# Two-layer diffusion backbone with PEER experts: decoding by 16-bit folds, gate one-hots by four-token comparisons

## Chip, cores and metric

The kernel runs on one core of a Trainium2 chip. The metric is device time in microseconds (us) of one execution; the time before is the median of three runs. The five engines of the core are called PE (matrix products, with PEld for its weight loads), DVE (vector), ACT (scalar and activation), POOL (general purpose) and SP (issues most DMAs).

## What is computed

Two layers over 512 latent and 256 context tokens of width 1024. Each layer has an attention and recurrent mixer, which the change leaves alone, and then a feed-forward part in which each token picks, for each of 8 heads, 16 of 16,384 experts:

```python
def peer_ffn(h, w_query, subkeys1, subkeys2, expert_u, expert_v):
    q = (h @ w_query).reshape(B, L, PEER_HEADS, 2, PEER_HALF)
    s1 = jnp.einsum('blhd,kd->blhk', q[..., 0, :], subkeys1)
    s2 = jnp.einsum('blhd,kd->blhk', q[..., 1, :], subkeys2)
    v1, i1 = lax.top_k(s1, PEER_TOPK)        # 16 of 128 rows
    v2, i2 = lax.top_k(s2, PEER_TOPK)        # 16 of 128 columns
    cand_score = v1[..., :, None] + v2[..., None, :]
    cand_index = i1[..., :, None] * N_KEYS + i2[..., None, :]
    top_score, top_pos = lax.top_k(cand_score, PEER_TOPK)
    expert_idx = jnp.take_along_axis(cand_index, top_pos, axis=-1)
    gates = jax.nn.softmax(top_score, axis=-1)
    ...
    act = gelu(einsum('td,ted->te', h_blk, expert_u[i_blk]))
    out = einsum('te,ted->td', g_blk * act, expert_v[i_blk])
```

Layer 0 does this for 4 blocks of 128 latent tokens and 2 of context tokens, layer 1 for the 4 latent blocks alone.

## The kernel before

**Two ways to the experts.** Some token blocks are *dense*: all 16,384 experts are computed for them with matrix products, and a gate matrix that is zero nearly everywhere picks what counts (the 4 latent blocks in layer 0, 3 of them in layer 1). The other blocks are *gathered*: POOL fetches one row of the expert table per token and step (L1285), and DVE multiplies it (L1297, and L1310 for the second table). Gather steps are strewn among all the rest.

**Choosing and decoding (`topk2`).** For each block, DVE finds the best 16 of 54 candidate pairs for each head and has their positions (`txf`). `decode` turns positions into expert numbers, two heads a call, four calls a block, 40 calls in the program: ACT spreads the positions (`tte`, L1220), DVE compares them with 0 to 53 (`toe`, L1225), multiplies by the candidates' numbers, which gives one nonzero in each row of 54 (`toh`, 16-bit integers, L1226), and sums each of the 32 rows (`tef`, L1227).

**The gate stage.** For a dense block, `gprep` transposes the expert numbers, split into row and column, and the gates into `gT` (rows 0, 1 and 2 of `T3`). `gstep` then takes four tokens at a time: a one-hot `o1` of the row number, a one-hot `o2` of the column number times the gate, and a product `o2` by `o1` for each token on PE (`g_ps`, L1558), which ACT copies out (`Gs`, L1560) and SP writes to memory. `o1` is made by DVE in one comparison over four tokens on odd steps (L1547), and on even steps by ACT (four times Abs into `ohd`, L1552, and one Relu, L1553). `o2` is made by DVE, one instruction per token with comparison and multiplication in one (L1555). The trace calls both tiles `oh`. There are 128 steps in layer 0 and 96 in layer 1, with three buffers of each one-hot and two of `g_ps`.

**What runs beside it.** In the same stage PE computes the first table's product for the dense blocks (`u_ps`, L158): per step `ustep`, SP loads `raw`, ACT rounds it to `uhi` (L1470), DVE subtracts to get `ulo` (L1471), PE does 24 matrix products, ACT applies Gelu (`ga`, L1476). A function `merge` spreads these steps, the gate steps, the decoding of the next block and gather steps evenly, and a scheduler then orders each engine's instructions before the program runs. Each engine works through its list in that fixed order. Behind the gate stage comes the second table's product (`pa` and `po`, L158).

Of the kernel before, what the change touches and what calls it, by code (L numbers as in the profile page):

```python
# [10 lines left out]
F32 = mybir.dt.float32  # L11
# [5 lines left out]
AF = mybir.ActivationFunctionType  # L17
ALU = mybir.AluOpType
# [83 lines left out]
def body(ctx: ExitStack, tc: tile.TileContext, I: dict, out: bass.AP):  # L102
    nc = tc.nc
    V, A, G, PE, SP = nc.vector, nc.scalar, nc.gpsimd, nc.tensor, nc.sync
    mul, add, sub = ALU.mult, ALU.add, ALU.subtract
# [7 lines left out]
    def K(name):  # L113
        o, n = COFF[name]
        return cst[:, o:o + n]
# [1051 lines left out]
    def topk2(pool, rp, tvx, res):  # L1167
        v, ix = tvx
        vv = v.rearrange("p (h f) k -> p h f k", f=2)
        w = {}  # L1170

        def prep():
            ixf = pool.tile([128, 16, 16], F32, name="tixf")
            V.tensor_copy(ixf, ix)
            iv = ixf.rearrange("p (h f) k -> p h f k", f=2)
            i1s = pool.tile([128, 8, 16], F32, name="ti1")
            V.tensor_scalar(i1s, iv[:, :, 0, :], 128.0, None, op0=mul)
            cd = w["cd"] = pool.tile([128, 8, NCAND], F32, name="tcd")
            ci = pool.tile([128, 8, NCAND], F32, name="tci")
            at = 0  # L1180
            for a0, a1, n in SEGS:
                na = a1 - a0
                for dst, x1, x2 in ((cd, vv[:, :, 0], vv[:, :, 1]), (ci, i1s, iv[:, :, 1])):
                    G.tensor_tensor(dst[:, :, at:at + na * n].rearrange("p h (a b) -> p h a b", b=n),
                                    x1[:, :, a0:a1, None].to_broadcast([128, 8, na, n]),
                                    x2[:, :, None, 0:n].to_broadcast([128, 8, na, n]), op=add)
                at += na * n
            w["ci"] = pool.tile([128, 8, NCAND], I16, name="tcj")
            A.copy(w["ci"], ci)

        def top():
            w["tv"] = pool.tile([128, 8, 16], F32, name="ttv")
            w["tx"] = pool.tile([128, 8, 16], U32, name="ttx")
            w["c2"] = pool.tile([128, 8, NCAND], F32, name="tc2")
            for h in range(8):
                V.max(out=w["tv"][:, h, 0:8], in_=w["cd"][:, h, :])

        def top2():
            for h in range(8):
                V.max_index(out=w["tx"][:, h, 0:8], in_max=w["tv"][:, h, 0:8], in_values=w["cd"][:, h, :])  # L1200

        def top3():
            for h in range(8):
                V.match_replace(out=w["c2"][:, h, :], in_to_replace=w["tv"][:, h, 0:8], in_values=w["cd"][:, h, :],  # L1204
                                imm_value=NEG)

        def top4():
            for h in range(8):
                V.max(out=w["tv"][:, h, 8:16], in_=w["c2"][:, h, :])

        def top5():
            for h in range(8):
                V.max_index(out=w["tx"][:, h, 8:16], in_max=w["tv"][:, h, 8:16], in_values=w["c2"][:, h, :])  # L1213
            w["txf"] = pool.tile([128, 8, 16], F32, name="ttxf")
            V.tensor_copy(w["txf"], w["tx"])
            w["ef"] = pool.tile([128, 128], F32, name="tef")

        def spread(h):
            te = w["te", h] = pool.tile([128, 2, 16, NCAND], BF, name="tte", bufs=2)
            A.copy(te, w["txf"][:, h:h + 2, :, None].to_broadcast([128, 2, 16, NCAND]))  # L1220

        def decode(h):
            oe = pool.tile([128, 2, 16, NCAND], BF, name="toe", bufs=1)
            oh = pool.tile([128, 2, 16, NCAND], I16, name="toh", bufs=1)
            V.tensor_tensor(oe, io16[:, None, None, :].to_broadcast([128, 2, 16, NCAND]), w["te", h], op=ALU.is_equal)  # L1225
            V.tensor_tensor(oh, oe, w["ci"][:, h:h + 2, None, :].to_broadcast([128, 2, 16, NCAND]), op=mul)  # L1226
            V.tensor_reduce(w["ef"][:, 16 * h:16 * h + 32].rearrange("p (h j) -> p h j", j=16), oh,  # L1227
                            axis=AX.X, op=add)

        def gates():  # L1230
            g = rp.tile([128, 8, 16], F32, name="gate")
            tv = w["tv"]
            V.tensor_tensor(g, tv, tv[:, :, 0:1].to_broadcast([128, 8, 16]), op=sub)
            A.activation(g, g, AF.Exp)
            sm = pool.tile([128, 8], F32, name="tsm")
            V.tensor_reduce(sm, g, axis=AX.X, op=add)
            V.reciprocal(sm, sm)
            V.tensor_tensor(g, g, sm[:, :, None].to_broadcast([128, 8, 16]), op=mul)
            res["g"] = g.rearrange("p h k -> p (h k)")

        def index():
            eidx = res["e"] = rp.tile([128, 128], I32, name="eidx")
            V.tensor_copy(eidx, w["ef"])

        return [prep, top, top2, top3, top4, top5, lambda: spread(0), gates, lambda: (spread(2), decode(0)), lambda: (spread(4), decode(2)),
                lambda: (spread(6), decode(4)), lambda: decode(6), index]

    def ffn_rows(L, r, mk):
# [80 lines left out]
    def tail(L, cat, last, ro, need_ctx):  # L1329
# [61 lines left out]
        op = eo.enter_context(tc.tile_pool(name=f"op{l}", bufs=1, side="right"))  # L1391
# [109 lines left out]
        wp = e1.enter_context(tc.tile_pool(name=f"pt{l}", bufs=1, side="right"))  # L1501
# [35 lines left out]
        def gstep(q, b, t0):  # L1537
            T3 = R[b]["T3"]
            if t0 % GTC == 0:
                R["Gs"] = gsp.tile([128, 128, GTC], F32, name="Gs")  # L1540
            Gs = R["Gs"]
            gp = pp.tile([128, 4, 128], F32, name="g_ps", tag="q_ps", bufs=2)
            o1 = wp.tile([128, 4, 128], F32, name="oh1", bufs=3)
            o2 = wp.tile([128, 4, 128], F32, name="oh2", bufs=3)
            io = K("iota")
            if (t0 // 4) % 2:
                V.tensor_tensor(o1, io[:, None, :].to_broadcast([128, 4, 128]),  # L1547
                                T3[:, 0, t0:t0 + 4, None].to_broadcast([128, 4, 128]), op=ALU.is_equal)
            else:
                od = wp.tile([128, 4, 128], F32, name="ohd", bufs=2)  # L1550
                for t in range(4):
                    A.activation(od[:, t, :], io, AF.Abs, scale=-1.0, bias=T3[:, 0, t0 + t:t0 + t + 1])  # L1552
                A.activation(o1, od, AF.Relu, scale=-1.0, bias=1.0)  # L1553
            for t in range(4):
                V.tensor_scalar(o2[:, t, :], io, T3[:, 1, t0 + t:t0 + t + 1], T3[:, 2, t0 + t:t0 + t + 1],  # L1555
                                op0=ALU.is_equal, op1=mul)
            for t in range(4):
                PE.matmul(gp[:, t, :], o2[:, t, :], o1[:, t, :], start=True, stop=True)  # L1558
            tl = t0 % GTC
            A.copy(Gs[:, :, tl:tl + 4], gp.rearrange("p t i -> p i t"))  # L1560
            if tl + 4 == GTC:
                SP.dma_start(gscr[(128 * q + t0) // GTC], Gs)

        seq = []
        for q, b in enumerate(dn):
            if q == 0:
                seq += topk2(wp, wp, tk[b], R[b])
            if q == 0 and gl:
                for c in gl:
                    seq += topk2(wp, gr, tk[c], R[c]) + [lambda c=c: gather(c)]  # L1570
            nxt = topk2(wp, wp, tk[dn[q + 1]], R[dn[q + 1]]) if q + 1 < nd else []
            gs = [lambda b=b: gprep(b)] + [lambda q=q, b=b, t=t: gstep(q, b, t) for t in range(0, 128, 4)]
            k = len(gs) // (len(nxt) + 1)
            for i, f in enumerate(gs):
                seq.append(f)
                if nxt and i % k == k - 1:
                    seq.append(nxt.pop(0))
            seq += nxt
# [202 lines left out]
```

## Time and profile before

| what | value |
|---|---|
| three runs | 4742.24, 4747.82 (median), 4757.47 us |
| the profiled execution | 4753.17 us, of which 4751.4 us span |
| busy share of the span | PE 90%, DVE 76%, ACT 41%, POOL 29% |
| gate stage of layer 0, first to last `g_ps` | 1121.1 to 1471.0 us |
| gate stage of layer 1 | 3616.0 to 3905.2 us |

The shares are means over stages with different limits, so the view to read is busy time by stretch: an engine that is busy through a whole stretch holds the others up there, and one that has gaps can take more work at no cost. Instructions overlap by some hundredths of a us on DVE and ACT, so the cost of one is read best from the distance between two starts in the timeline. The clock granted to PE is given as a share of 2.4 GHz.

### The profile page before, as it was taken

To read this page: it belongs to the slowest core of one execution; us is meant where nothing else is said; L and a number is where in the kernel's file an instruction comes from. 1 tells how busy PE (TensorE), PEld (TensorE's weight loads), DVE (VectorE), ACT (ScalarE), POOL (GpSimd) and SP (SyncE) were. 2 spreads that over 40 slices of the span, in tenths; PEclk is the share of its full clock that TensorE was granted. 3 is DMA by queue.
4 is the path that set the end of the run, shared out by engine and by line. 5 is a ranking of instruction groups with operands and counts; after the bars stand their busy time and mean duration, and the time that the engine had idled before them with its cause. 6 is when DMAs were issued, how large, how long until landed. Compare 5 with 4: busy or idle time off the path is not lost. (4 is left out here: it accounts for less than half of the span.)

```text
span 4751.4 us, 85354 instructions
## 1 busy us (share of the span) xinstructions
PE 4288.6 (90%) x32715; PEld 3568.5 (75%) x32715; DVE 3619.3 (76%) x7842; ACT 1952.0 (41%) x3407; POOL 1366.7 (29%) x1256
## 2 busy tenths in 40 slices
PE   6998688877999999988899989868898999999999
PEld 4664576766787887767687778457678997899998
DVE  3457675899997888877788746766589967888885
ACT  3355343436674232222222234644336763333332
POOL 0201002442222345555455221200222102244441
PEclk8999898998999999999999999989899999999999
DMA  6656415435779999988898632651525769999995
GB/s 242 236 178 196 103 39 192 160 124 186 253 264 330 333 321 330 316 302 295 288 330 317 236 123 85 203 132 30 175 90 192 255 249 332 345 330 336 333 326 209
DMA packets 576904, 1106.71 MB, mean 233 GB/s; under 512 B 145328, under 2 KB 358000, under 8 KB 566768
## 3 DMA queue, kind: packets, MB, share of 16 engines
q1 hardware_dynamic: 465904, 698.56, 43.0%
q0 software_dynamic: 110592, 402.70, 23.6%
q8 instruction: 257, 4.21, 0.4%
q14 instruction: 151, 1.24, 0.1%
HBM read 960.37 MB, written 140.74 MB: 232 GB/s over the span
## 5 line engine op out<-in xcount | busy, mean ns | idle before, releaser
L158 PE MATMUL u_ps<-phi,uhi 128*128 128x512 f32 (+1 forms) x2048 | 765.1, 374 | 65.2 <-ACT ga L1476 48.4
L1285 POOL DMA_INDIRECT u<-in_u,eidx x384 | 485.7, 1265 | 1173.1 <-DVE u L1297 836.0
L158 PE MATMUL u_ps<-phi,ulo 128*128 128x512 f32 (+1 forms) x2048 | 757.3, 370 | 34.1 <-DVE ulo L1471 34.1
L158 PE MATMUL u_ps<-plo,uhi 128*128 128x512 f32 (+1 forms) x2048 | 753.3, 368 | 0.0
L1285 POOL DMA_INDIRECT u<-in_v,eidx x384 | 517.7, 1348 | 518.1 <-DVE gacc L1310 434.5
L1470 ACT CAST uhi<-raw 128x1024 fp32r<-128x1024 f32 x256 | 269.0, 1051 | 933.9 <-PE u_ps L158 546.6
L158 PE MATMUL pa<-vhi,whi 128*128 128x512 f32 x1536 | 601.5, 392 | 10.5 <-ACT whi L149 10.5
L158 PE MATMUL pa<-vlo,whi 128*128 128x512 f32 x1536 | 601.2, 391 | 0.0
L158 PE MATMUL pa<-vhi,wlo 128*128 128x512 f32 x1536 | 600.9, 391 | 0.0
L1297 DVE SCALAR_TENSOR_TENSOR u<-u,gh 128x1024 f32<-128x1024 f32 x384 | 468.3, 1230 | 120.2 <-DMA u<-in_u,eidx 112.4
L1310 DVE SCALAR_TENSOR_TENSOR gacc<-u,gw,gacc 128x1024 f32<-128x1024 f32 x381 | 488.4, 1282 | 93.3 <-DMA u<-in_v,eidx 89.8
L158 PEld LDWEIGHTS u_ps<-phi,uhi 128*128 128x128 f32 x2048 | 392.6, 192 | 120.2 <-ACT ga L1476 58.6
L158 PEld LDWEIGHTS u_ps<-phi,ulo 128*128 128x128 f32 x2048 | 391.3, 191 | 81.0 <-DVE ulo L1471 38.9
L158 PEld LDWEIGHTS u_ps<-plo,uhi 128*128 128x128 f32 x2048 | 392.2, 192 | 44.2
L1471 DVE TENSOR_TENSOR ulo<-raw,uhi 128x1024 fp32r<-128x1024 f32 x256 | 313.8, 1226 | 143.4 <-ACT uhi L1470 139.6
L149 ACT CAST whi<-w 128x512 fp32r<-128x512 f32 (+1 forms) x256 | 145.5, 568 | 601.3 <-DVE w L1618 384.0
L158 PEld LDWEIGHTS pa<-vhi,whi 128*128 128x128 f32 x1536 | 290.4, 189 | 69.8 <-issue 10.8
L158 PEld LDWEIGHTS pa<-vhi,wlo 128*128 128x128 f32 x1536 | 289.9, 189 | 61.4
L158 PEld LDWEIGHTS pa<-vlo,whi 128*128 128x128 f32 x1536 | 290.2, 189 | 58.7
L1604 DVE TENSOR_TENSOR vlo<-vraw,vhi 128x1024 fp32r<-128x1024 f32 x256 | 312.3, 1220 | 27.7 <-ACT vhi L1603 27.6
L1603 ACT CAST vhi<-vraw 128x1024 fp32r<-128x1024 f32 x256 | 263.7, 1049 | 66.4 <-PE pa L158 37.6
L1555 DVE TENSOR_SCALAR oh<-cst,gT 128x128 f32<-128x128 f32 x896 | 254.1, 362 | 0.6 <-ACT gT L1535 0.5
(867 smaller groups left out, 8603.8 us busy)
## 6 DMA issues: line engine op xcount, KB each, us to landing
raw<-in_ut SPq DMA_DIRECT2D x256, 512.0 KB
vraw<-in_v SPq DMA_DIRECT2D x256, 512.0 KB
gscr<-Gs SPq DMA_DIRECT2D x28, 2048.0 KB
mod_w<-in_mod_w SPq DMA_DIRECT2D x48, 1024.0 KB
Gt<-gscr SPq DMA_DIRECT2D x32, 1024.0 KB
raw<-in_w_q SPq DMA_DIRECT2D x48, 512.0 KB
Gt<-gscr SPq DMA_DIRECT2D x32, 768.0 KB
wo<-in_w_out SPq DMA_DIRECT2D x40, 512.0 KB
```

Source lines behind the costliest of these rows:

```text
L149: A.copy(hi, src)
L158: PE.matmul(ps, a, b, start=first and q == 0 and j == 0, stop=last and q == n - 1 and j == 2)
L1285: G.indirect_dma_start(out=t, out_offset=None, in_=I[f"{tab}{l}"], in_offset=bass.IndirectOffsetOnAxis(ap=res["e"][:, e:e + 1], axis=0))
L1297: V.scalar_tensor_tensor(u, u, 1.0, c["h"], op0=mul, op1=mul, accum_out=c["act"][:, e:e + 1])
L1310: V.scalar_tensor_tensor(acc, v, w[:, e:e + 1], acc, op0=mul, op1=add)
L1470: A.copy(uhi, ut)
L1471: ins = V.tensor_tensor(ulo, ut, uhi.bitcast(F32), op=sub)
L1555: V.tensor_scalar(o2[:, t, :], io, T3[:, 1, t0 + t:t0 + t + 1], T3[:, 2, t0 + t:t0 + t + 1], op0=ALU.is_equal, op1=mul)
L1603: A.copy(r["vhi"], vt)
L1604: gafter(V.tensor_tensor(r["vlo"], vt, r["vhi"].bitcast(F32), op=sub), f)
```

## The change

Two places change. In `decode`, the 54 columns of `toh` are folded before the sum: columns 28 to 53 are added onto columns 0 to 25, then 14 to 27 onto 0 to 13, in place and in 16-bit integers, and the sum runs over 14 columns in place of 54. In `gstep`, both one-hots are made by DVE in one comparison over four tokens each, on every step, and ACT multiplies `o2` by the gates in place, one instruction per token; the Abs and Relu steps and the tile `ohd` are gone.

```diff
--- before.py
+++ after.py
@@ -1224,7 +1224,9 @@
             oh = pool.tile([128, 2, 16, NCAND], I16, name="toh", bufs=1)
             V.tensor_tensor(oe, io16[:, None, None, :].to_broadcast([128, 2, 16, NCAND]), w["te", h], op=ALU.is_equal)
             V.tensor_tensor(oh, oe, w["ci"][:, h:h + 2, None, :].to_broadcast([128, 2, 16, NCAND]), op=mul)
-            V.tensor_reduce(w["ef"][:, 16 * h:16 * h + 32].rearrange("p (h j) -> p h j", j=16), oh,
+            V.tensor_tensor(oh[:, :, :, 0:26], oh[:, :, :, 0:26], oh[:, :, :, 28:54], op=add)
+            V.tensor_tensor(oh[:, :, :, 0:14], oh[:, :, :, 0:14], oh[:, :, :, 14:28], op=add)
+            V.tensor_reduce(w["ef"][:, 16 * h:16 * h + 32].rearrange("p (h j) -> p h j", j=16), oh[:, :, :, 0:14],
                             axis=AX.X, op=add)
 
         def gates():
@@ -1542,18 +1544,11 @@
             gp = pp.tile([128, 4, 128], F32, name="g_ps", tag="q_ps", bufs=2)
             o1 = wp.tile([128, 4, 128], F32, name="oh1", bufs=3)
             o2 = wp.tile([128, 4, 128], F32, name="oh2", bufs=3)
-            io = K("iota")
-            if (t0 // 4) % 2:
-                V.tensor_tensor(o1, io[:, None, :].to_broadcast([128, 4, 128]),
-                                T3[:, 0, t0:t0 + 4, None].to_broadcast([128, 4, 128]), op=ALU.is_equal)
-            else:
-                od = wp.tile([128, 4, 128], F32, name="ohd", bufs=2)
-                for t in range(4):
-                    A.activation(od[:, t, :], io, AF.Abs, scale=-1.0, bias=T3[:, 0, t0 + t:t0 + t + 1])
-                A.activation(o1, od, AF.Relu, scale=-1.0, bias=1.0)
+            io = K("iota")[:, None, :].to_broadcast([128, 4, 128])
+            V.tensor_tensor(o2, io, T3[:, 1, t0:t0 + 4, None].to_broadcast([128, 4, 128]), op=ALU.is_equal)
+            V.tensor_tensor(o1, io, T3[:, 0, t0:t0 + 4, None].to_broadcast([128, 4, 128]), op=ALU.is_equal)
             for t in range(4):
-                V.tensor_scalar(o2[:, t, :], io, T3[:, 1, t0 + t:t0 + t + 1], T3[:, 2, t0 + t:t0 + t + 1],
-                                op0=ALU.is_equal, op1=mul)
+                A.activation(o2[:, t, :], o2[:, t, :], AF.Copy, scale=T3[:, 2, t0 + t:t0 + t + 1])
             for t in range(4):
                 PE.matmul(gp[:, t, :], o2[:, t, :], o1[:, t, :], start=True, stop=True)
             tl = t0 % GTC
```

The orders of the instructions change with it between the first decode call and the end of the gate stage of each layer, and nowhere else. On DVE, in the middle of layer 0's gate stage, before (L1555 and L1547 make `oh`, L1225 to L1227 are a decode call, L1297 is a gather step):

```order
L1225 TENSOR_TENSOR toe<-io_62,tte 128x1728
L1547 TENSOR_TENSOR oh_13438<-cst,gT_12847 128x512
L1226 TENSOR_TENSOR toh<-toe,tcj 128x1728
L1555 TENSOR_SCALAR oh_13439<-cst,gT_12847 128x128
L1227 TENSOR_REDUCE tef<-toh 128x32
L1555 TENSOR_SCALAR oh_13439<-cst,gT_12847 128x128 x3
L1297 SCALAR_TENSOR_TENSOR u,gact<-u,gh 128x1024
L1555 TENSOR_SCALAR oh_13455<-cst,gT_12847 128x128 x4
L1225 TENSOR_TENSOR toe<-io_62,tte 128x1728
L1547 TENSOR_TENSOR oh_13479<-cst,gT_12847 128x512
```

and at the same decode call after (L1548 and L1549 make the two one-hots, L1227 and L1228 are the folds, L1229 the sum):

```order
L1225 TENSOR_TENSOR toe<-io_62,tte 128x1728
L1548 TENSOR_TENSOR oh_13477<-cst,gT_12871 128x512
L1226 TENSOR_TENSOR toh<-toe,tcj 128x1728
L1549 TENSOR_TENSOR oh_13476<-cst,gT_12871 128x512
L1227 TENSOR_TENSOR toh<-toh 128x32x26
L1299 SCALAR_TENSOR_TENSOR u,gact<-u,gh 128x1024
L1228 TENSOR_TENSOR toh<-toh 128x32x14
L1548 TENSOR_TENSOR oh_13529<-cst,gT_12871 128x512
L1229 TENSOR_REDUCE tef<-toh 128x32
L1549 TENSOR_TENSOR oh_13528<-cst,gT_12871 128x512
```

The two comparisons of a step stand between the parts of the decode call where the single-token ones stood. On ACT, at the same place, before (L1552 and L1553 make a one-hot, L1560 copies a gate product out, L1470 and L1476 belong to the product `u_ps`):

```order
L1470 CAST uhi<-raw 128x1024
L1476 ACTIVATE ga<-u_ps 128x512
L1560 COPY Gs<-g_ps 128x128x4 x2
L1553 ACTIVATE oh_13530<-ohd 128x512
L1220 CAST tte<-ttxf 128x1728
L1552 ACTIVATE ohd<-cst,gT_12847 128x128 x4
L1560 COPY Gs<-g_ps 128x128x4
L1553 ACTIVATE oh_13568<-ohd 128x512
L1552 ACTIVATE ohd<-cst,gT_12847 128x128 x4
```

and after (L1551 multiplies by the gates; L1555, L1472 and L1478 are L1560, L1470 and L1476 of before):

```order
L1555 COPY Gs<-g_ps 128x128x4
L1551 ACTIVATE oh_13477<-oh_13477,gT_12871 128x128
L1555 COPY Gs<-g_ps 128x128x4
L1551 ACTIVATE oh_13477<-oh_13477,gT_12871 128x128 x3
L1472 CAST uhi<-raw 128x1024
L1555 COPY Gs<-g_ps 128x128x4
L1551 ACTIVATE oh_13529<-oh_13529,gT_12871 128x128 x4
L1220 CAST tte<-ttxf 128x1728
L1551 ACTIVATE oh_13552<-oh_13552,gT_12871 128x128 x4
```

The multiplications, which wait for DVE's comparison of the same step and are waited for by PE, now stand ahead of `uhi` and between the copies of gate products, where instructions stood that waited for neither.

## Rows read from the trace of the kernel before

**Rows 1.** Busy time by stretch (us, instructions), granted clock, DMA; the columns stand first.
```profile
core 0: us, PE busy (x) PEld busy (x) DVE busy (x) ACT busy (x) POOL busy (x), PEclk, DMA share, GB/s
936.00:1060.00 124.00, 101.14 (x460) 81.29 (x458) 123.97 (x528) 44.46 (x55) 56.15 (x34) 0.94 0.35 117
1060.00:1121.00 61.00, 28.96 (x105) 22.32 (x105) 60.46 (x241) 19.94 (x26) 21.32 (x31) 0.69 0.47 150
1121.10:1400.00 278.90, 258.48 (x1456) 221.17 (x1457) 278.19 (x795) 202.97 (x412) 63.69 (x63) 0.98 0.68 246
1400.00:1471.00 71.00, 71.00 (x442) 62.59 (x440) 63.18 (x173) 56.10 (x129) 16.29 (x11) 1.00 0.75 286
3560.00:3616.00 56.00, 42.93 (x195) 39.72 (x194) 53.74 (x159) 34.51 (x46) 10.12 (x20) 0.82 0.31 107
3616.00:3800.00 184.00, 178.01 (x1165) 176.13 (x1164) 179.40 (x482) 137.99 (x271) 37.12 (x35) 0.99 0.71 256
3800.00:3905.20 105.20, 105.20 (x718) 103.93 (x718) 76.13 (x201) 75.11 (x162) 5.31 (x4) 1.00 0.63 240
```

**Rows 2.** DVE timeline at 1444 us: start, us, engine, line, operation, count.
```profile
1444.14 0.69 DVE L1547 TENSOR_TENSOR oh<-cst,gT 128x512 f32<-128x512 f32 x1
1444.75 2.15 DVE L1555 TENSOR_SCALAR oh<-cst,gT 128x128 f32<-128x128 f32 x8
1446.79 0.70 DVE L1547 TENSOR_TENSOR oh<-cst,gT 128x512 f32<-128x512 f32 x1
```

**Rows 3.** Groups by line, 1121.1 to 1400: busy us, mean ns | idle before, releaser.
```profile
L1555 DVE TENSOR_SCALAR oh<-cst,gT 128x128 f32<-128x128 f32 x378 | 109.6, 365 | 0.0
...
L1547 DVE TENSOR_TENSOR oh<-cst,gT 128x512 f32<-128x512 f32 x47 | 32.6, 694 | 0.7 <-PE g_ps L1558 0.7
```

**Rows 4.** Groups by line, 3616 to 3800.
```profile
L1555 DVE TENSOR_SCALAR oh<-cst,gT 128x128 f32<-128x128 f32 x225 | 64.3, 358 | 0.0
...
L1547 DVE TENSOR_TENSOR oh<-cst,gT 128x512 f32<-128x512 f32 x28 | 19.3, 688 | 0.2 <-PE g_ps L1558 0.2
```

**Rows 5.** DVE timeline in one decode call, 968.79 us.
```profile
968.79 1.05 DVE L1226 TENSOR_TENSOR toh<-toe,tcj 128x1728 int16<-128x1728 bf16 x1
969.74 0.30 DVE L1150 MAX8 tv<-s_sb 128x8 f32<-128x128 f32 x1
969.95 1.95 DVE L1227 TENSOR_REDUCE tef<-toh 128x32 f32<-128x1728 int16 x1
971.80 0.29 DVE L1150 MAX8 tv<-s_sb 128x8 f32<-128x128 f32 x1
```

**Rows 6.** DVE groups by line ahead of layer 0's gate stage (936 to 1121).
```profile
L1226 DVE TENSOR_TENSOR toh<-toe,tcj 128x1728 int16<-128x1728 bf16 x12 | 20.5, 1709 | 0.0
...
L1225 DVE TENSOR_TENSOR toe<-io,tte 128x1728 bf16<-128x1728 bf16 x12 | 14.4, 1203 | 0.0
```

**Rows 7.** ACT timeline at 1311.65 us.
```profile
1311.65 1.27 ACT L1552 ACTIVATE ohd<-cst,gT 128x128 f32<-128x128 f32 x4
1312.82 0.62 ACT L1553 ACTIVATE oh<-ohd 128x512 f32<-128x512 f32 x1
1313.34 0.57 ACT L1560 COPY Gs<-g_ps 128x512 f32<-128x512 f32 x1
```

**Rows 8.** What PE waited for, 1121.1 to 1400: us, times, longest.
```profile
PE g_ps L1558 <- DVE oh L1555: 9.9, 9, 1.6
PE u_ps L158 <- DVE ulo L1471: 4.6, 7, 1.1
PE g_ps L1558 <- ACT oh L1553: 3.2, 4, 1.2
PE g_ps L1558 <- ACT Gs L1560: 2.2, 3, 0.8
```

**Rows 9.** The gate products on PE by line, 1400 to 1471.
```profile
L1558 PE MATMUL g_ps<-oh,oh 128*128 128x128 f32 x264 | 34.0, 280 | 0.0
```

**Rows 10.** The gate products on PE by line, 3800 to 3905.2.
```profile
L1558 PE MATMUL g_ps<-oh,oh 128*128 128x128 f32 x330 | 42.0, 278 | 0.0
```

## Prediction

> **What bounds the kernel now.** I read busy time by stretch first, because the change touches only the decode calls and the two gate stages, and shares of the whole span (PE 90%, DVE 76%) say nothing about those. The columns to compare are PE and DVE [rows 1]. From 936 to 1121 us, ahead of layer 0's gate stage, DVE is busy for 184.4 of 185 us and PE for 130.1: DVE is the bound. From 1121 to 1400, DVE is busy for 278.2 of 278.9 us and PE for 258.5, so DVE is the bound and PE has 20.4 us of gaps. From 1400 to 1471, PE is busy throughout and DVE is not: PE is the bound, and a faster DVE is worth nothing. In layer 1, DVE leads ahead of the stage (53.7 of 56 us, PE 42.9), both are nearly full from 3616 to 3800 (DVE 179.4 of 184, PE 178.0), and from 3800 on PE alone is full. Second, the waits of PE where DVE bounds layer 0: 9.9 us for DVE's one-hots, 4.6 for `ulo`, which is also DVE's, and 5.4 for ACT's one-hots and copies [rows 8]. So most gaps of PE there are DVE's, but some are ACT's already.
>
> All terms below come from the profiled execution (4753.17 us, span 4751.4, so 1.8 us lie outside the span). The median of the three runs is 4747.82, that is 5.4 us shorter; I take the differences off the median.
>
> **Gates on DVE.** In the timeline two starts give what an instruction occupies: the four-token comparison 0.61 us (1444.14 to 1444.75), eight single-token ones 2.04 us, or 0.255 each [rows 2]. Two steps took 2.04 + 0.61 = 2.65 us; four comparisons take 2.44. Each pair of steps saves 0.21 us. There are 47 pairs from 1121 to 1400 [rows 3], which is 9.9 us, and 28 pairs from 3616 to 3800 [rows 4], which is 5.9 us. Both comparisons have the shape and operands of one that the trace has, so little is unknown here.
>
> **Gates on ACT.** A pair of steps held four Abs and one Relu: 1.17 us (1311.65 to 1312.82) and 0.52 us (to 1313.34), together 1.69 [rows 7]. Eight multiplications by a per-partition operand, at the 0.29 us of one Abs of the same shape, make 2.34. That adds 0.65 us a pair, 31 us from 1121 to 1400, where ACT was busy for 203 us of 279. The whole of it is covered as long as PE and DVE set the pace: ACT would be at 234 of about 266 us, 88%. What is not covered is the new wait: the multiplication sits in ACT's list behind DVE's comparison, and `uhi`, `ga` and the copies out of PE's buffers are queued behind it. PE waits for all of these. The trace shows 5.4 us of such waits on ACT at 73% busy [rows 8]; with 88% I take 3 us more in this stretch, between 0 and the whole of the gain.
>
> **Decode.** The sum over 54 columns occupies 1.85 us (969.95 to 971.80), the 16-bit multiplication over the same 1728 elements 0.95 us (968.79 to 969.74) [rows 5]. The 512 elements at 0.61 us and 1728 at 1.85 give 1.02 ns an element and a fixed 0.09 us at the slower rate; the 0.95 us gives 0.50 ns at the faster one. The new sum over 448 elements is then 0.55 us. The folds, 832 and 448 elements, are 0.50 and 0.31 us if 16-bit additions in rows of 26 and 14 run like the 16-bit multiplication, 0.94 and 0.55 if like the sum. A call saves 0.49 us or loses 0.19. I take the gain, because the multiplication is the nearest row: it too takes two 16-bit inputs and writes integers. By the order of DVE there are 12 calls ahead of layer 0's gate stage, 12 in it, 6 ahead of layer 1's and 10 in it.
>
> There is a second cost. From 936 to 1121 the multiplication took 1709 ns on average and `toe` 1203 [rows 6], against 1.05 us in the quiet call [rows 5], a mean of 1.46 against 1.05: two-input instructions are stretched by 0.39 while POOL, busy there for 56 of the first 124 us [rows 1], works beside them. The folds are such instructions too: 12 calls of 0.81 us stretched by 0.39 give back 3.8 us of 5.9. Ahead of layer 0's stage 2 us remain.
>
> **The sum.** Ahead of layer 0's stage: 2 us. From 1121 to 1400: 9.9 + 12 of 0.49 = 15.8 us of relief on DVE, less than PE's gaps of 20.4, minus 3 for ACT: 13. From 1400 to 1471: 0. Ahead of layer 1's stage: 6 of 0.49 = 2.9, of which 2.5, since DVE is not quite full. From 3616 to 3800: relief of 5.9 + 10 of 0.49 = 10.8, but PE has gaps of only 6.0; I take half of these, 3. From 3800: 0. Together 20.5, about 21 us: 4747.8 - 21 = 4727. What is late next is PE, in both stages. Behind the stages the order of every engine is as before, so that the time gained stays. The bounds: if every gap of PE that DVE causes goes, 5.9 + 20.4 + 2.9 + 6.0 = 35 us, 4713. If the folds run at the slower rate and collide as above, the decode terms turn into a loss of some 11 (40 calls of 0.19 and 3.8), and of the gates 9.9 - 3 and 5.9 remain: a gain of 2 us, 4746.
>
> **Rivals.** *PE and its order take over.* In the static order PE's products stand in a row fixed before the run; where DVE is early, the next product may wait for something else (`uhi` behind the multiplications). For it: PE has no gaps in 176 us of the 639 of the two stages, and 6 in the next 184 [rows 1]. Against it: the largest waits of PE in layer 0 name DVE. Then only the calls ahead of the stages and a quarter of the 15.8 count: 8 us, 4740.
>
> *ACT becomes the bound: slower.* Each step's `o2` must now pass DVE, ACT and PE in turn. Where PE has no gaps, a multiplication that comes late holds PE directly: 33 steps from 1400 to 1471 (264 recorded products, 8 a step [rows 9]) and 41 from 3800 [rows 10]. One more multiplication's time, 0.29 us [rows 7], on each of these 74 steps is 21 us; with the same on the 55 steps from 3616 to 3800, 37 us. If the gain in layer 0's bounded stretch is lost as well and only the 5 us ahead of the stages stay, the time is 4764 to 4780. It decides once ACT's list runs later than the three buffers of `o2` can hide, that is, when ACT nears the pace of PE; for it speaks the 88%, against it that `o1` was made on ACT on every other step already and cost PE 3.2 us [rows 8].
>
> The Trainium skill has a rule for this: its page "ScalarE: Activation LUTs", section "Rules for kernel authors", tells authors to use VectorE and not ScalarE for a multiplication. By it this half of the change goes the wrong way and the slower rival holds; no run here shows that yet.
>
> *Collisions or slow folds.* If the folds run at the sum's rate, or the added two-input instructions collide with POOL in the gate stage as ahead of it, most is given back. Against it: in the gate stage, with POOL at 63.7 of 278.9 us [rows 1], the comparisons took 694 ns [rows 3], hardly over the 688 of layer 1 [rows 4]. 4746, as above.
>
> The Trainium skill's "GPSIMD Engine Reference", section "1. Specifications", says that POOL shares its SBUF interfaces with VectorE and that instructions with two SBUF inputs contend. By it the four-token comparisons, which have two such inputs where the single-token ones had one, would be stretched by 0.39 of 0.61 us whenever POOL is at work, 23% of this stretch, or 10 us for its 188 comparisons; the 694 ns speak against that.
>
> *More than the sum.* All gaps go, as in the bound: 4713. PE's clock, granted at 0.69 and 0.82 ahead of the stages where PE has long gaps [rows 1], could come up with it.
>
> **How the numbers follow.** A measurement of this kernel tells about 0.3% from no change, 14 us. Forecast (gain of 11 to 30 us): 0.48, of which 0.08 below 14 us. More than the sum: 0.12. PE takes over: 0.18. Collisions or slow folds: 0.08. ACT, slower: 0.14, of which 0.03 within 14 us. Faster: 0.40 + 0.12 = 0.52. Same: 0.08 + 0.18 + 0.08 + 0.03 = 0.37. Slower: 0.11. The predicted time is the forecast's, 4727. The range runs from 4710, just under the largest gain, to 4757: it takes in the forecast, the two small-gain cases and the mild end of the slower one, and leaves out the rest of that and a little below, some 0.15.
>
> **What the profile after would show.** Right: the two folds near 0.5 and 0.3 us and the sum near 0.55 us; the comparisons near 0.69 us; layer 0's gate stage, first to last gate product, down from 350 to about 337 us; layer 1's from 289 to about 286; PE's waits for DVE's `oh` mostly gone. Wrong: waits of PE for ACT's `oh` or `uhi` of tens of us (the slower rival); folds near 0.9 us, or well over that while POOL works (the third); a gate stage of unchanged length with DVE idle and PE waiting elsewhere (the first).

## The result and the profile after

The changed kernel takes 4721.05 us (median of 5 runs, 4717.52 to 4727.79) beside 4747.82 (5 runs, 4742.24 to 4760.98) of the kernel before. The ratio is 0.9947, with a 95% interval of 0.9933 to 0.9960: faster by 19 to 32 us, where 21 was forecast. The profiled execution took 4727.79 us, of which 4725.6 is span, against 4753.17 and 4751.4.

Busy time by stretch, changed kernel; the stretches are from the first decode call to the first gate product of layer 0, layer 0's gate stage, the same up to 1380, the stretch from the first decode call of layer 1 to its first gate product, and layer 1's gate stage.

```profile
core 0: us, PE busy (x) PEld busy (x) DVE busy (x) ACT busy (x) POOL busy (x), PEclk, DMA share, GB/s
930.70:1107.70 177.00, 125.64 (x548) 99.71 (x546) 175.91 (x771) 60.78 (x75) 75.24 (x61) 0.86 0.40 131
1107.70:1446.90 339.20, 328.40 (x1900) 279.55 (x1899) 320.87 (x676) 302.26 (x737) 90.02 (x73) 1.00 0.72 262
1107.50:1380.00 272.50, 262.24 (x1493) 222.35 (x1492) 268.37 (x595) 239.23 (x570) 80.82 (x66) 1.00 0.72 259
3542.60:3590.70 48.10, 37.55 (x188) 35.80 (x187) 46.34 (x154) 28.89 (x34) 9.94 (x15) 0.88 0.32 114
3590.70:3882.00 291.30, 284.82 (x1880) 280.37 (x1878) 239.41 (x452) 246.61 (x586) 48.49 (x39) 0.99 0.68 248
```

The same two gate stages in the kernel before (columns as above):

```profile
1121.10:1470.90 349.80, 329.38 (x1894) 283.66 (x1895) 341.27 (x967) 258.97 (x541) 79.99 (x73) 0.98 0.70 254
3616.10:3905.00 288.90, 282.92 (x1879) 279.76 (x1878) 255.44 (x682) 212.90 (x432) 42.43 (x39) 0.99 0.68 250
```

Layer 0's gate stage is 10.6 us shorter. PE does the same work in it (329.4 and 328.4 us), so what went is idle time of PE: 20.4 us before, 10.8 after. DVE lost 20.4 us of work there and ACT gained 43.3. Up to 1380 DVE is busy for 268.4 of 272.5 us and ACT for 239.2, or 88%. Layer 1's gate stage did not get shorter, though DVE has 16 us less to do in it.

What PE waited for in layer 0's gate stage, changed kernel (us, times, longest); it answers to [rows 8]:

```profile
PE g_ps L1553 <- ACT oh L1551: 5.7, 10, 1.5
PE g_ps L1553 <- DVE oh L1549: 2.0, 2, 1.0
PE u_ps L158 <- ACT uhi L1472: 1.6, 4, 0.4
PE u_ps L158 <- DVE ulo L1473: 0.6, 2, 0.3
```

The 9.9 and 4.6 us for DVE are down to 2.0 and 0.6, and the largest wait is now for ACT's multiplications, 5.7.

DVE's groups by line in the same stage (busy us, mean ns, then idle before), changed kernel; the sum answers to the 1.85 us of [rows 5], the comparisons to [rows 3]:

```profile
L1548 DVE TENSOR_TENSOR oh<-cst,gT 128x512 f32<-128x512 f32 x127 | 87.2, 686 | 4.4 <-PE g_ps L1553 3.8
...
L1226 DVE TENSOR_TENSOR toh<-toe,tcj 128x1728 int16<-128x1728 bf16 x12 | 12.6, 1052 | 0.0
...
L1229 DVE TENSOR_REDUCE tef<-toh 128x32 f32<-128x448 int16 x12 | 7.3, 612 | 0.0
L1227 DVE TENSOR_TENSOR toh<-toh 128x832 int16<-128x832 int16 x12 | 7.0, 585 | 0.0
L1228 DVE TENSOR_TENSOR toh<-toh 128x448 int16<-128x448 int16 x12 | 4.6, 386 | 0.0
```

From start to start a fold of 832 elements occupies 0.49 us, one of 448 takes 0.31, and the sum 0.53, read at the places below. That is the faster of the two rates the prediction weighed.

**Where the time went, over three profiles of each kernel.** One profile of each is not enough here: code that is the same in both differs by several us from run to run. So I profiled both again (the last experiment). The table has the means of three.

| stretch | forecast | before | after | difference |
|---|---|---|---|---|
| start to the first decode call (same code) | 0 | 938.2 | 935.1 | -3.1 |
| first decode call to layer 0's first `g_ps` | -2 | 181.2 | 176.8 | -4.4 |
| layer 0's gate stage | -13 | 350.2 | 339.4 | -10.8 |
| between the layers' parts (same code) | 0 | 2096.0 | 2092.1 | -3.9 |
| layer 1: first decode call to first `g_ps` | -2.5 | 50.9 | 48.8 | -2.1 |
| layer 1's gate stage | -3 | 288.6 | 290.9 | +2.3 |
| behind it (same code) | 0 | 844.1 | 844.4 | +0.3 |
| span | -20.5 | 4749.2 | 4727.6 | -21.6 |

The stretches that the change touches give 15.0 us. The other 6.7 lie in code that is the same in both. The 2.1 us ahead of layer 1's gate stage are no more than the spread there: the three profiles after have 48.1, 50.2 and 48.2 us.

### The profile page after: what moved, and what is told of

The parts are those of the page before. It is cut to its first block, busy times and chain, and to the rows that moved or that the text cites. A ratio compares the mean times of both kernels' runs of the same rounds, so it can differ in the third digit from the quotient of the medians.

```text
span 4725.6 us, 85317 instructions
## 1 busy us (share of the span) xinstructions
PE 4282.3 (91%) x32715; PEld 3561.5 (75%) x32715; DVE 3575.7 (76%) x7362; ACT 2020.3 (43%) x3743; POOL 1382.4 (29%) x1256
## 3 DMA queue, kind: packets, MB, share of 16 engines
q1 hardware_dynamic: 465904, 698.56, 43.3%
q14 instruction: 150, 1.23, 0.1%
## 5 line engine op out<-in xcount | busy, mean ns | idle before, releaser
L1472 ACT CAST uhi<-raw 128x1024 fp32r<-128x1024 f32 x256 | 268.1, 1048 | 798.3 <-PE u_ps L158 432.8
L158 PEld LDWEIGHTS pa<-vlo,whi 128*128 128x128 f32 x1536 | 290.2, 189 | 58.8
L1551 ACT ACTIVATE oh<-oh,gT 128x128 f32<-128x128 f32 x896 | 287.9, 396 | 49.7 <-DVE oh L1548 49.1
```

What stands on the lines that cost most here:

```text
L158: PE.matmul(ps, a, b, start=first and q == 0 and j == 0, stop=last and q == n - 1 and j == 2)
L1472: A.copy(uhi, ut)
L1551: A.activation(o2[:, t, :], o2[:, t, :], AF.Copy, scale=T3[:, 2, t0 + t:t0 + t + 1])
```

## The experiments

The first four shared one chip and its runs of the kernel before, 4751.89 us; the next four another set, 4750.7; then 4747.93. "Stage" is from the first to the last gate product.

The scheduler orders the instructions of each of these kernels anew, so two kernels can differ in the order as well as in the edit. I count the order by the number of `u_ps` products that stand ahead of each of layer 0's 512 gate products on PE. With POOL quiet, with rounded products and with each half where it seemed to pay, it is that of the changed kernel for all 512. Without the multiplication it is so for 289, with one more for 275, without the row one-hot for 276, with the folds alone for 298 and with the gates alone for 377. In these five, what the edit costs and what the other order costs are not told apart.

**One half alone: the folds.** The gates are those of the kernel before.

```diff
+            V.tensor_tensor(oh[:, :, :, 0:26], oh[:, :, :, 0:26], oh[:, :, :, 28:54], op=add)
+            V.tensor_tensor(oh[:, :, :, 0:14], oh[:, :, :, 0:14], oh[:, :, :, 14:28], op=add)
...
```

> Only the decode folds; the gate one-hots as before. Forecast's theory (relief on DVE becomes time where DVE bounds): 2 to 5 us ahead of layer 0's gate stage, 6 in it, 3 to 5 ahead of layer 1's, 2 or 3 in it: 13 to 19 us faster than before, with layer 0's gate stage at 344 us in place of 350. Rival (the gates' comparisons carry the whole): under 6 us faster.

4728.85 us, ratio 0.9955 (0.9938 to 0.9971). Stages 343.7 and 286.2 us, and 175.6 ahead of layer 0's. That is 23 us faster where 13 to 19 were expected; layer 0's stage is the 344 us expected. By the stretches of the change, against the means of before, it is 16 us, and the rest lies in code that is the same.

**The other half alone: the gates.** `gstep` as changed, the sum over 54 columns as before.

```diff
-            V.tensor_tensor(oh[:, :, :, 0:26], oh[:, :, :, 0:26], oh[:, :, :, 28:54], op=add)
-            V.tensor_tensor(oh[:, :, :, 0:14], oh[:, :, :, 0:14], oh[:, :, :, 14:28], op=add)
...
```

> Only the gate one-hots; the decode sums all 54 columns as before. Forecast's theory: 7 us less in layer 0's gate stage (343 us), 0 to 3 in layer 1's, nothing ahead of the stages: 5 to 10 us faster than before. Rival (PE caps the gain, so that either half alone reaches nearly the whole): 15 us or more in the stages alone, and the two halves add to well over the whole. Rival (ACT costs): slower than before by 5 us or more.

4739.11 us, ratio 0.9978 (0.9968 to 0.9989). Stages 347.2 and 287.3 us, and 182.3 ahead of layer 0's. The time is 12.8 us less where 5 to 10 were expected, but layer 0's stage gave 3 us (against the mean of before) and not 7.

**The whole again**, unaltered, beside the halves.

> The changed kernel unaltered, once more beside the kernel before on one chip. The stretches that the change touches gave 20.6 us in the traces, the medians 27. If the trace's sum is right: 18 to 24 us faster. If the 8 us that the profiled run was ahead of the first decode call belong to the change: 25 to 30 us faster, and its trace again is about 8 us ahead there.

4731.42 us, ratio 0.9959 (0.9944 to 0.9974). Stages 339.2 and 290.0 us. That is 20.5 us faster, and the first decode call starts at 935.2 us, so the 8 us did not come again. Counted from the first decode calls, the first pair of profiles gives 16.4 us in the stretches of the change, not the 20.6 of the expectation.

Busy time in layer 0's gate stage with the folds alone, and with the gates alone:

```profile
1107.30:1451.00 343.70, 327.62 (x1900) 281.28 (x1899) 335.33 (x992) 258.47 (x541) 76.61 (x73) 1.00 0.73 258
```
```profile
1117.20:1464.40 347.20, 332.31 (x1894) 281.64 (x1895) 327.70 (x652) 301.16 (x737) 91.46 (x74) 1.00 0.71 256
```

On DVE the halves are worth what the sum gave them: 341.3 down to 335.3 is 5.9 us for the folds, and down to 327.7 is 13.6 for the gates (64 pairs of 0.21 are 13.4). Together they are 20.4. In the stage's length the folds' 5.9 became 6.1, and the gates' 13.6 became 2.6. Put on top of the folds, the gates give 4.5 more (343.7 to 339.2). What PE waits for with the gates alone shows a part of why:

```profile
PE g_ps L1551 <- ACT oh L1549: 8.1, 15, 1.3
PE g_ps L1551 <- DVE oh L1547: 2.1, 2, 1.2
PE u_ps L158 <- ACT uhi L1470: 1.3, 3, 0.4
```

The wait for DVE's one-hots, 9.9 us before, is down to 2.1, and one of 8.1 for ACT's multiplication stands in its place. PE is also busy for 2.9 us more than before (332.3 for 329.4); why is open. In time, the whole (0.9947, 0.9959) can't be told from the folds alone (0.9955).

**ACT's part taken away.** The multiplication by the gates is left out.

```diff
-            for t in range(4):
-                A.activation(o2[:, t, :], o2[:, t, :], AF.Copy, scale=T3[:, 2, t0 + t:t0 + t + 1])
```

> The changed kernel without ACT's multiplication by the gates (512 and 384 instructions of 0.29 us gone; the products use bare one-hots, so the gates are left out of the dense experts). Forecast's theory: ACT's cover holds, only PE's waits for its one-hots (5.7 us in layer 0, 1.8 in layer 1) go: 5 to 10 us faster than the changed kernel. Rival (the multiplication on ACT sets the pace in the stages): 20 us faster or more.

4730.01 us, ratio 0.9956 (0.9942 to 0.9970): it can't be told from the changed kernel's 4731.42 in the same set, where 5 to 10 us were expected. Stages 336.4 and 289.5 us. ACT's load falls to half, and PE waits for DVE again (busy time, then what PE waited for):

```profile
1110.20:1446.60 336.40, 322.08 (x1900) 277.29 (x1899) 319.96 (x676) 155.38 (x227) 90.70 (x73) 1.00 0.73 264
```
```profile
PE g_ps L1551 <- DVE oh L1549: 10.2, 11, 1.8
PE u_ps L158 <- DVE ulo L1473: 3.8, 4, 1.6
```

So with the multiplication layer 0's stage is 2.8 us longer (339.2 against 336.4), though it is 147 us of work on ACT there, and PE's idle time does not vanish with it: it goes back to DVE.

**One more multiplication on ACT.** The fourth token of every step is multiplied twice.

```diff
             for t in range(4):
                 A.activation(o2[:, t, :], o2[:, t, :], AF.Copy, scale=T3[:, 2, t0 + t:t0 + t + 1])
+            A.activation(o2[:, 3, :], o2[:, 3, :], AF.Copy, scale=T3[:, 2, t0 + 3:t0 + 4])
```

> The changed kernel with one more multiplication by the gate per step on ACT (the fourth token's gate enters twice): 0.29 us a step, the price that the slower rival put on each step. If ACT's load is still covered, as it seems without the multiplication (hardly any change): under 6 us slower than the changed kernel. If ACT is at its edge (302 + 37 us of layer 0's gate stage of 339): 10 to 20 us slower, mostly in layer 0. Slower rival as put: 21 to 37 us slower.

4744.71 us, ratio 0.9987 (0.9971 to 1.0004): the gain is gone. Layer 0's stage takes 357.3 us, 18 more; layer 1's 289.8, none more. Busy time in layer 0's stage, then what PE waited for:

```profile
1111.40:1468.70 357.30, 336.72 (x1904) 284.63 (x1903) 324.25 (x676) 338.73 (x865) 88.16 (x73) 0.99 0.70 249
```
```profile
PE u_ps L158 <- ACT uhi L1472: 6.7, 9, 1.3
PE u_ps L158 <- DVE ulo L1473: 5.1, 6, 1.2
PE g_ps L1554 <- ACT oh L1551: 4.1, 6, 1.3
PE g_ps L1554 <- ACT Gs L1556: 3.5, 7, 1.0
```

The 128 extra instructions are 36 us of work for ACT, whose 302 us in a stage of 339 had just room for them on paper; an engine with gaps could not take more work at no cost here. PE waits for everything that is queued on ACT (`uhi`, one-hots, copies), and for `ulo`, which DVE makes from `uhi`. These are the waits that the slower rival told of. They are not the whole of the 18 us: PE's idle time grew by 9.8 (10.8 to 20.6), and PE is also busy for 8.3 more, whose cause is open. In layer 1 ACT got as full, and nothing was lost:

```profile
3601.40:3891.20 289.80, 284.15 (x1880) 278.56 (x1879) 238.64 (x450) 271.62 (x675) 49.34 (x39) 1.00 0.69 250
```

So a full ACT alone does not make the loss; how much of it is the other order is not shown.

**DVE relieved further.** The row one-hot is replaced by a constant tile, so that DVE makes one comparison a step.

```diff
...
-            V.tensor_tensor(o1, io, T3[:, 0, t0:t0 + 4, None].to_broadcast([128, 4, 128]), op=ALU.is_equal)
...
-                PE.matmul(gp[:, t, :], o2[:, t, :], o1[:, t, :], start=True, stop=True)
+                PE.matmul(gp[:, t, :], o2[:, t, :], K("iota"), start=True, stop=True)
```

> The changed kernel without the comparison for the row one-hot (the products use a constant in its place, so the gate matrix is not the reference's): 0.61 us of DVE a step gone, 78 us in layer 0's gate stage and 59 in layer 1's. If PE caps the stages: layer 0's gate stage from 339 to 326 to 333 us, layer 1's from 290 to about 286, 10 to 17 us faster than the changed kernel. If DVE still bounds layer 0's: 30 us faster or more.

4725.16 us, ratio 0.9943 (0.9927 to 0.9960): it can't be told from the changed kernel (0.9947, 0.9959), where 10 to 17 us were expected. Busy time in layer 0's stage:

```profile
1108.70:1443.40 334.70, 325.11 (x1903) 278.85 (x1901) 246.93 (x548) 301.52 (x738) 79.76 (x73) 0.99 0.74 266
```

DVE has 74 us less to do than in the changed kernel, and the stage is 4.5 us shorter; layer 1's is unchanged (289.4). In this order, DVE's time beyond the change is worth next to nothing: PE is busy for 325 of 335 us.

**POOL's subtraction taken out of the way.** Ahead of layer 0's gate stage POOL subtracts to get the low parts of a weight (`ulo`, L152, 13 times). Here ACT copies a tile in its place.

```diff
-                qs = peer_query(L, lat, hhi, hlo, wtiles, xp, q_bank, s_bank, tk, lambda i: G)
+                qs = peer_query(L, lat, hhi, hlo, wtiles, xp, q_bank, s_bank, tk, lambda i: A)
...
+        if eng_lo is A:
+            A.copy(lo, src)
...
```

> The changed kernel with POOL's 16 subtractions ahead of layer 0's gate stage taken away (ACT writes a plain copy in their place, so the queries' low parts are wrong). If DVE's two-input instructions are held while POOL's own two-input instruction runs: no fold, product or comparison there over 1.2 us, and 5 to 9 us less ahead of the stage (four held instructions of 1.5 to 2.2 us, and held gather steps). If the long ones have another cause: they stay.

4713.18 us, ratio 0.9926 (0.9907 to 0.9944). The stretch ahead of layer 0's gate stage takes 162.7 us in place of 177.0, 14.3 less where 5 to 9 were expected; both gate stages stay (339.2 and 290.2). What happens there is seen in the changed kernel's timeline (start, duration), first POOL, then DVE:

```profile
1002.19 2.55 POOL L152 TENSOR_TENSOR ulo<-raw,uhi 128x1024 fp32r<-128x1024 f32 x1
...
1015.98 3.06 POOL L152 TENSOR_TENSOR ulo<-raw,uhi 128x1024 fp32r<-128x1024 f32 x1
```
```profile
1002.53 2.66 DVE L1227 TENSOR_TENSOR toh<-toh 128x832 int16<-128x832 int16 x1
...
1005.31 0.38 DVE L1228 TENSOR_TENSOR toh<-toh 128x448 int16<-128x448 int16 x1
1005.62 1.21 DVE L1299 SCALAR_TENSOR_TENSOR u<-u,gh 128x1024 f32<-128x1024 f32 x1
1006.76 0.61 DVE L1229 TENSOR_REDUCE tef<-toh 128x32 f32<-128x448 int16 x1
1007.29 0.86 DVE L1150 MAX8 tv<-s_sb 128x8 f32<-128x128 f32 x4
...
1015.25 0.58 DVE L1227 TENSOR_TENSOR toh<-toh 128x832 int16<-128x832 int16 x1
1015.74 1.05 DVE L1225 TENSOR_TENSOR toe<-io,tte 128x1728 bf16<-128x1728 bf16 x1
1016.70 2.58 DVE L1228 TENSOR_TENSOR toh<-toh 128x448 int16<-128x448 int16 x1
...
1031.71 2.29 DVE L1245 CAST eidx<-tef 128x128 int32<-128x128 f32 x1
```

The fold of 0.58 us that starts at 1002.53, while POOL's subtraction runs, ends at 1005.19, or 0.45 us after that subtraction; a fold of 0.38 us takes 2.58 beside a later subtraction and ends 0.24 us after it. The fold at 1005.31, with no subtraction running, is not held. The last line is an instruction with one input that usually takes 0.21 us: it starts 0.18 us after another subtraction of POOL's (1031.53, 2.39 us) and is held too. With POOL's subtractions gone, no decode instruction is held (DVE's group of the larger fold in that stretch):

```profile
L1230 DVE TENSOR_TENSOR toh<-toh 128x832 int16<-128x832 int16 x12 | 7.0, 583 | 0.0
```

**The gate products halved on PE.** Both one-hots are made in a rounded type, for which PE has one recorded product a token, not two.

```diff
-            o1 = wp.tile([128, 4, 128], F32, name="oh1", bufs=3)
-            o2 = wp.tile([128, 4, 128], F32, name="oh2", bufs=3)
+            o1 = wp.tile([128, 4, 128], F32R, name="oh1", bufs=3)
+            o2 = wp.tile([128, 4, 128], F32R, name="oh2", bufs=3)
...
-                A.activation(o2[:, t, :], o2[:, t, :], AF.Copy, scale=T3[:, 2, t0 + t:t0 + t + 1])
+                A.activation(o2[:, t, :], o2[:, t, :].bitcast(F32), AF.Copy, scale=T3[:, 2, t0 + t:t0 + t + 1])
```

> The changed kernel with both one-hots in the rounded 32-bit format of the other products, so that PE does one pass in place of two recorded ones for each token (gates rounded in it). PE would lose up to 0.12 us of 0.24 a token: 61 us in layer 0's gate stage and 46 in layer 1's. If PE caps the stages: layer 0's to DVE's 321 us or somewhat above, layer 1's to 250 to 265: 40 to 55 us faster than the changed kernel. If the stages hang on the chain over DVE and ACT and not on PE's work: under 15 us.

4735.18 us, ratio 0.9969 (0.9954 to 0.9983). Neither expectation came: it is no faster than the changed kernel (0.9947, 0.9959). Layer 0's stage is 354.8 us, 16 longer than in the changed kernel, with half of the gate products' records and the same order; layer 1's is 286.6. Busy time in both stages:

```profile
1109.00:1463.80 354.80, 316.07 (x1388) 250.16 (x1387) 321.32 (x675) 297.51 (x735) 89.49 (x73) 0.89 0.70 250
3598.70:3885.30 286.60, 260.43 (x1496) 249.59 (x1494) 239.39 (x452) 243.10 (x586) 48.58 (x39) 0.96 0.71 252
```

The granted clock is 0.89 where the changed kernel had 1.00. PE's timeline shows what a fall looks like:

```profile
1407.57 0.50 PE L158 MATMUL u_ps<-phi,uhi 128*128 128x512 f32 x1 [0.28 <-ACT uhi L1472]
...
1408.83 0.77 PE L1553 MATMUL g_ps<-oh,oh 128*128 128x128 f32 x2 [0.53 <-ACT oh L1551]
...
1412.16 0.63 PE L158 MATMUL u_ps<-plo,uhi 128*128 128x512 f32 x1
1412.59 0.63 PE L158 MATMUL u_ps<-phi,ulo 128*128 128x512 f32 x1
...
1416.31 0.40 PE L158 MATMUL u_ps<-plo,uhi 128*128 128x512 f32 x1
1416.54 0.39 PE L158 MATMUL u_ps<-phi,ulo 128*128 128x512 f32 x1
```

After waits of 0.28 and 0.53 us the same product starts every 0.43 us, and from 1415 on every 0.23; the granted clock after the waits is 0.50 of full speed, the lower level of 1.2 GHz, though PE is busy without a gap by then (busy time, columns as above):

```profile
1410.00:1412.50 2.50, 2.50 (x8) 2.08 (x7) 2.50 (x5) 2.50 (x7) 0.20 (x1) 0.50 0.98 416
```

So with the halved work came longer waits and a slower clock. That one follows from the other is not shown; this run tells only that they came together.

**Each half where it seemed to pay.** Folds everywhere, the comparisons in layer 0 alone.

```diff
+            if l == 0:
...
+                V.tensor_tensor(o2, io, T3[:, 1, t0:t0 + 4, None].to_broadcast([128, 4, 128]), op=ALU.is_equal)
...
+            else:
...
+                    A.activation(o1, od, AF.Relu, scale=-1.0, bias=1.0)
```

> The folds everywhere, the four-token comparisons in layer 0's gate stage alone; layer 1's gates are those of before. If the comparisons pay only where DVE bounds a stage and cost a little where PE does, layer 0's gate stage takes 339 us as in the changed kernel and layer 1's 286 as with the folds alone, and the time is 4 us under both, a ratio of 0.993 to 0.995. If the 4 to 5 us of layer 1 between the two kernels are variation between runs, layer 1's stage comes out at 289 to 291 again, and the ratio equals the changed kernel's (0.995).

4727.03 us, ratio 0.9950 (0.9937 to 0.9964): no faster than the changed kernel. Both stages:

```profile
1116.50:1455.60 339.10, 328.26 (x1900) 279.52 (x1900) 320.88 (x676) 302.21 (x737) 89.95 (x73) 1.00 0.72 262
3595.10:3883.90 288.80, 283.46 (x1880) 280.85 (x1879) 248.46 (x685) 212.30 (x432) 40.54 (x39) 0.99 0.71 250
```

Layer 0 is as expected. Layer 1's stage, with the very code of the folds alone, takes 288.8 where that run had 286.2; so 2 or 3 us there can be variation between runs, and there was not much to win.

**Both kernels profiled again.**

> The kernel before, unaltered, with a profile of its own. Open: in the profile of before the first decode call starts at 938.9 us, in the later ones of changed kernels between 930.7 and 936.3, though everything up to there is the same code. If that is variation between runs, this profile too starts it somewhere in 930 to 939 and its stretches are as in the first one within 2 us (182 ahead of layer 0's gate stage, 350 in it, 51 and 289 in layer 1). If the change reaches back (by the transfers in flight or the clock), the first call starts at 938 or later again. Time ratio 1.000 within 0.002.

> The kernel before, unaltered, a third profile. Open: the start of the first decode call, up to which all kernels have the same code, was 938.9 and 937.8 us in two profiles of before, and 930.7 to 938.4 in ten of changed kernels. If that is variation between runs, a third profile of before falls anywhere from 930 to 939, most likely under 937. If the change reaches back, it starts at 937 or later again.

> The changed kernel, unaltered, a third profile, for the same question. If it is variation, the first decode call starts anywhere from 930 to 939 us (930.7 and 935.2 so far); if the change reaches back, at 936 or sooner. In either case layer 0's gate stage takes 339 us, the stretch ahead of it 177 to 179, and layer 1's stage 290 to 291.

The kernel before took 4747.47 us again (ratio 0.9995, 0.9983 to 1.0006). The first decode call started at 938.9, 937.8 and 937.9 us in the kernel before, and at 930.7, 935.2 and 939.4 in the changed one. A changed kernel can start it as late as any of before, so the 3.1 us by which the means differ are not shown to belong to the change. Ahead of layer 0's gate stage the changed kernel's third profile has 174.9 us, under the 177 to 179 expected. Within the changed stretches the profiles agree within 1 us in layer 0's stage (349.8 to 350.5, and 339.2 to 339.9), 4 ahead of it, and 1.4 in layer 1's (288.1 to 288.9, and 290.0 to 291.4). Of the last, the 2.3 us between the means are more than the spread of either kernel's three, but less than the 2.6 by which the same code differed in two runs above: that the change made layer 1's stage longer is likely and not shown, and that it made it no shorter stands.

## Why the prediction was right, and where not

The time, 4721 for 4727, and the direction were right, and the mechanism is the one told: DVE bounded two stretches, was relieved, and PE is late next. By the table, though, the changed stretches give 15 us, not 20.5, and the rest of the 22 lies in code that the change leaves alone. So that the total came out as close as it did is in part luck; several of its terms did not.

- **What the instructions cost.** The folds at 0.49 and 0.31 us and the sum at 0.53, for 0.50, 0.31 and 0.55; the comparisons 686 ns, for 690; DVE's relief in layer 0's stage 20.4 us, for 0.21 by 64 pairs and 0.49 by 12 calls, which are 19.3. Choosing the multiplication as the row nearest to the folds was right.
- **Layer 0's gate stage: 10.8 for 13.** The deduction of 3 us for ACT agrees in size with the 2.8 us by which the stage is shorter without the multiplication. What failed is that the rest of DVE's relief before 1400 would all become time. With ACT out of the way the stage is 13.8 us shorter than before with 21.3 of relief, and 74 us more of relief on the changed kernel bring 4.5. That is the first rival (PE and its order), at a part of its size. The folds' relief became time whole and the gates' hardly. That the gates moved work to the engine that PE waits for next is one reason, as the 8.1 us of waits for ACT show; but without the multiplication only 2.8 us come back of the 11 that are missing (13.6 less 2.6). The rest lies with PE and the order, and no run takes these apart.
- **Ahead of layer 0's gate stage: 4.4 for 2.** The step that added a stretch of 0.39 us for every fold to the holds of before was wrong. An instruction is either held until a subtraction of POOL's is over or not at all, and the 13 subtractions held DVE for about as long in both kernels, whatever they met. Against the run with POOL quiet, DVE's groups of instructions took 13.6 us more in the changed kernel's first profile (4.1 of it the folds, 2.7 the multiplications, 2.8 the gather steps, 4.0 two CASTs) and 13.4 in the kernel before (7.9 the multiplications). The folds were held for about the 3.8 us counted, but in the place of others.
- **Ahead of layer 1's: 2.1 for 2.5.** Near, by luck. The prediction counted 6 decode calls there and 10 in the stage; in the trace of the kernel before, 8 stand ahead of the first gate product and 8 behind it. By these the relief is 3.9 us, not 2.9.
- **Layer 1's gate stage: +2.3 for -3.** Wrong. PE had gaps of 6 us before, nearly all for DVE, and has 6.5 after, 4.0 of them for ACT. Before, then after:

```profile
PE u_ps L158 <- DVE ulo L1471: 4.0, 3, 2.5
PE g_ps L1558 <- DVE oh L1555: 1.7, 1, 1.7
```
```profile
PE g_ps L1553 <- ACT Gs L1555: 2.2, 4, 0.8
PE g_ps L1553 <- ACT oh L1551: 1.8, 2, 1.6
PE g_ps L1553 <- DVE oh L1549: 1.0, 1, 1.0
```

  Taking half of PE's gaps as gain had no row behind it. Here the rival of PE and its order held, which gave this stage nothing. Why PE is also busy for 1.9 us more in these two profiles is open.
- **The slower rival.** It did not come. The run with one extra multiplication, in its own order, lost 18 us in layer 0 for 0.29 us a step. Of these, 8.6 came in the last 32 steps, near the rival's price for those (33 steps by 0.29, 10 us), and 9.5 in the steps ahead, which the rival left free. In layer 1 the same extra cost nothing, though ACT was busy for 271.6 of 289.8 us, where the rival counted 12 us and more.
- **The two rules cited.** The Trainium skill's "ScalarE: Activation LUTs", section "Rules for kernel authors", would have kept the multiplication off ScalarE. Here layer 0's stage is 2.8 us longer with it than without, where the gates' half took 13.6 us off DVE and made the stage 2.6 us shorter; with one more multiplication a step it was 18 us longer again. So this stage speaks weakly against the rule, and for it once more such work is put on ACT. The contention that the Trainium skill's "GPSIMD Engine Reference", section "1. Specifications", names is in the trace, ahead of the gate stage. In that stage it hardly shows (the longest comparison took 0.89 us, the mean 0.69), probably for a reason the prediction missed: 73 of POOL's 90 us there are issues of gathers, and no subtraction of L152 is among the rest.

## What to carry to other kernels

Relief of the bound engine is worth what the next engine in line leaves of it: when the work is moved and not removed, look up how full the engine is that receives it, and who waits for that one. Where a stage has two engines near full, price an edit by PE's idle time there, and take no share of it without a row that says whose it is. When the expected gain is under 1%, profile both kernels more than once and compare stretch by stretch, since code that nobody touched moved by as much as a third of the gain. And where a scheduler sets the order, see how much of the order an experiment kept before its time is called the price of the edit.

## What the runs showed that was not expected

- A fold that starts while POOL subtracts two 128x1024 tiles waits until POOL is done and then takes its usual time: 2.66 us for 0.58, 2.58 for 0.38. Having two inputs is not the only thing that decides it: the sum and MAX8, with one input, were not seen held, but the CAST of `eidx`, also with one, took 2.29 us for 0.21. The 13 subtractions ahead of layer 0's gate stage cost 14.3 us of 177, some 1.1 us each; that is about what DVE would need for such a subtraction itself (1.23 us for the same shape in the gate stage), so by this estimate moving them there would win nothing.
- With less work for PE its stage was longer: with half of the gate products' records and the same order, 354.8 us for 339.2, at a granted clock of 0.89 for 1.00. What ties these together is open.
